# Weight granules 8 to 55 split by casting and accumulating loads from GpSimd's queue, with a ScalarE negation between

## The chip, the cores and the metric

The kernel runs on one core of one Trainium2 chip. The metric is device time in microseconds of one execution. In this document PE is the matrix engine (TensorE), PEld its weight load, DVE the vector engine (VectorE), ACT the scalar engine (ScalarE), POOL the GpSimd engine, and SP the engine (SyncE) whose queue issues the loads and stores of the kernel before.

## The reference

One decoder layer on 512 positions of width 1024, all in float32: a Mamba-2 block (`ssd_mixer`) and a sparse attention (`nsa_mixer`) side by side, an output projection with a residual, a gated feed-forward part with a short convolution, and a last RMSNorm. Cut to what matters here:

```python
h = rms_norm(x, norm1_g)
p = h @ w_in                       # 1024 x 5184: q, k, v, gates, SSM inputs
y = concat([ssd_mixer(...), rms_norm(nsa_mixer(...), attn_norm_g)])
x = x + y @ w_out                  # 2048 x 1024
u = causal_dwconv(rms_norm(x, norm2_g) @ ffn_w_up, ffn_conv_w, ffn_conv_b)
x = x + (silu(u[..., :FF]) * u[..., FF:]) @ ffn_w_down
out = rms_norm(x, final_norm_g)
```

Every product `h @ w` has to keep float32 accuracy.

## The kernel before, in words

Matmuls run on operands of type float32r. To keep the accuracy, each float32 operand `a` is split into `hi`, which is `a` written as float32r, and `lo = a - hi`, also float32r, and a product is three matmuls: hi·hi, lo·hi and hi·lo. For activations the split is made where they are computed; for weights it is made after the load.

The weights come in **granules** of 128 partitions x 1024 float32 (512 KB). The list `seq` (line 446) names 122 of them in the order of use: 0 to 39 are the input projection (`in_win`), 40 to 55 the output projection (`in_wout`), 56 to 121 the feed-forward part (`in_wup`, `in_wdn`). `w_load` (line 452) loads two granules in one 1 MB transfer on SP's queue into one of two `wr` buffers; the first two transfers go in four pieces of 256 KB between the pieces of the input. `w_split` (line 468) makes `wh` (a cast) and `wl` (a subtraction) of one granule; there are four buffers of each. `w_get` (line 483) is called by each job that multiplies with a granule, and records splits a few granules ahead.

The kernel is not written to the engines directly. Each operation is recorded (`Program.record`), and a planner (`Program.schedule`, line 284) then orders all operations with its own costs: it takes, over all engines, the operation that can start first, and among equals the one recorded first. Buffers are handed out in the order in which they were asked for. An operation recorded on `S` as a plain copy (a cast) may go to ACT or to DVE; one recorded on `DP` may go to DVE or to POOL. Line 390 is the helper that issues every planned operation, so all rows of the profile carry L390 and are told apart by their tiles. Each engine works through its own queue in the planned order, with semaphore waits for data and buffers.

The stages, by the time in the profiled execution: a start of some 40 us (granules 0 to 3, then the norm); projections with granules 4 to 11 and the compression of keys and values (40 to 100 us); attention woven with the projections of granules 12 to 39 (100 to 420 us); the SSD part woven with the first half of the output projection, tiles `on`, granules 40 to 47 (420 to 520 us); the second half, tiles `os`, granules 48 to 55 (520 to 567 us); the feed-forward part, tiles `psb` and `dn`, granules 56 to 121, to the end.

In the attention the tiles are: `pss` scores, `nm` row maxima, `p` probabilities, `l` and `rl` row sums and their inverses, `tb` transposed probabilities, `pth` and `ptl` their split, `ct` and `cp` the compressed branch, `o` the output in PSUM, `oT`, `oNh`, `oNl` the gathered and split output. `rx` and `rw` belong to the rotary embedding: `rw` is filled by four small transfers from `rx`.

The job of one output-projection half holds its four granules for four row tiles, so 2 x 4 x 3 = 24 matmuls use each granule:

```python
    def out_ssm(half):
        g0 = nxt(4)
        ws = [w_get(g0 + p_, 3 - p_) for p_ in range(4)]
        for t in range(NT):
            for g in range(2):
```

Of the kernel before, what the change touches and what calls it, by code (L numbers as in the profile page):

```python
# [10 lines left out]
F32 = mybir.dt.float32  # L11
# [8 lines left out]
P = 128  # L20
# [5 lines left out]
NEG = -1.0e30  # L26
N_SLOT = 57
N_EAGER = 3
# [135 lines left out]
class Program:  # L164


    def __init__(self, tc):
        self.tc, self.ops, self.first = tc, [], False
        self.pe, self.act, self.dve, self.pool, self.sp, self.dp = (
            _Engine(self, e) for e in ("PE", "ACT", "DVE", "POOL", "SP", "DP"))  # L170

    def buf(self, pool, shape, dt, name):
# [73 lines left out]
    def _cost(self, op, e, n, args, kw, ins, outs):  # L246
# [10 lines left out]
        if e == "ACT":  # L257
            extra = sum(isinstance(kw.get(x), View) for x in ("scale", "bias", "accum_out"))
            return ins[0].free / 1.2 + (52 if is_ps[0] else 94) + 93 * extra, TABLE.get(args[2].name, 0)
        if e in ("DVE", "POOL"):  # L260
            f = max([v.free for v in ins] + [outs[0].free])
# [21 lines left out]
    def schedule(self):  # L283
# [30 lines left out]
        while len(done) < n:  # L314
# [43 lines left out]
            if op.port.get(e):  # L358
                held[e] = op.end
            if e == "SP":  # L360
                dma_free = max(dma_free, t + 1300) + op.lat
                op.end = dma_free + 900
# [6 lines left out]
            for s in op.succ:  # L369
                s.ndep -= 1  # L370
                s.est = max(s.est, op.end + lat(e, next(iter(s.alts))))
                if s.ndep == 0:
                    push(s)
# [28 lines left out]
def layer_kernel(ctx: ExitStack, tc: tile.TileContext, x, xt, win, wdtg, wout, wup, wdn, pack, gcol, rows, cw1, consts, rot, out):  # L402
    pr = Program(tc)
    mm = pr.pe.matmul
    V, S, DP, PE, SP = pr.dve, pr.act, pr.dp, pr.pe, pr.sp

# [31 lines left out]
    raw, wh, wl = {}, {}, {}  # L438

    def w_load():  # L440
        p = st["load"]
        if 2 * p >= len(seq):
            return
        arr, i = seq[2 * p]
        raw[p] = alloc(wp, (P, 2, D), F32, f"wr{p}", "wr", 2)
        if p < 2:

            for z in range(4):
                load_x(4 * p + z)
                cs = slice(512 * (z % 2), 512 * (z % 2) + 512)  # L450
                SP.dma_start(raw[p][:, z // 2, cs], arr[p, :, z // 2, cs])
        else:
            SP.dma_start(raw[p], arr[i // 2])
        st["load"] += 1

    def w_split():
        i = st["split"]
        if i >= len(seq):
            return
        r = raw[i // 2][:, i % 2, :]  # L460
        wh[i] = alloc(wp, (P, D), F32R, f"wh{i}", "wh", 4)
        wl[i] = alloc(wp, (P, D), F32R, f"wl{i}", "wl", 4)
# [6 lines left out]
        if i % 2:  # L469
            del raw[i // 2]  # L470

    def w_get(i, ahead=2):
        while st["split"] <= i + ahead and st["split"] < len(seq):
            while st["load"] * 2 <= st["split"] + 1 and st["load"] * 2 < len(seq):
# [9 lines left out]
    def load_x(j):  # L484
        xT.append(slot(f"xT{j}"))
        SP.dma_start(xT[j], xt[j * P:(j + 1) * P])
# [11 lines left out]
    SP.dma_start(gT, gcol)  # L498
    w_load()
    ck = const("ck", (P, NCK), F32)  # L500
    SP.dma_start(ck[:, :P], consts[:, :P])
    w_load()
    SP.dma_start(ck[:, P:], consts[:, P:])
# [1078 lines left out]
```

## Time and profile before

| | |
|---|---|
| time before, median of 3 runs | 943.01 us (936.67 to 943.62) |
| the profiled execution's own time | 939.94 us |
| its span (first to last instruction) | 938.2 us, mean granted TensorE clock 0.987 |
| busy: PE / PEld / DVE / ACT / POOL | 894.1 / 727.9 / 756.8 / 408.5 / 77.4 us |
| read from HBM | 72.15 MB |

The share of busy time is an average over stages with different limits, so the tables below are read by stage. A busy PE is not a PE at its peak: matmuls are pipelined and one that waits for its operand behind others is counted as busy.

### The profile page before, as it was taken

To read this page: it belongs to the slowest core of one execution; us is meant where nothing else is said; L and a number is where in the kernel's file an instruction comes from. 1 tells how busy PE (TensorE), PEld (TensorE's weight loads), DVE (VectorE), ACT (ScalarE), POOL (GpSimd) and SP (SyncE) were. 2 spreads that over 40 slices of the span, in tenths; PEclk is the share of its full clock that TensorE was granted. 3 is DMA by queue.
4 is the path that set the end of the run, shared out by engine and by line. 5 is a ranking of instruction groups with operands and counts; after the bars stand their busy time and mean duration, and the time that the engine had idled before them with its cause. 6 is when DMAs were issued, how large, how long until landed. Compare 5 with 4: busy or idle time off the path is not lost.

```text
span 938.2 us, 12701 instructions
## 1 busy us (share of the span) xinstructions
PE 894.1 (95%) x4589; PEld 727.9 (78%) x4589; DVE 756.8 (81%) x1463; ACT 408.5 (44%) x933; POOL 77.4 (8%) x51
## 2 busy tenths in 40 slices
PE   9899889889998999999999999999999999999996
PEld 6777656767786798878777789888888888888886
DVE  7968999999999988888999678887774457777655
ACT  5434666667676677568667134312210001221013
POOL 0000222222201200010323001000000000000000
PEclk9999999999999999999999899999999999999999
DMA  9472211111111111131130222322223322222302
GB/s 308 154 202 81 72 52 56 57 51 62 46 57 57 45 45 46 46 114 56 34 136 1 90 90 90 135 90 89 90 90 99 113 101 91 90 90 93 105 28 90
DMA packets 19726, 80.82 MB, mean 86 GB/s; under 512 B 3152, under 2 KB 3920, under 8 KB 12112
## 3 DMA queue, kind: packets, MB, share of 16 engines
q1 hardware_dynamic: 19664, 80.02, 25.1%
q8 instruction: 36, 0.59, 0.3%
q14 instruction: 26, 0.21, 0.1%
HBM read 72.15 MB, written 2.10 MB: 79 GB/s over the span
## 4 chain that ended last, share of the span: by engine, by line
PE 70%; DVE 16%; ACT 6%; DMA 4%; issue 2%; SPq 1%; DVEq 0%; ACTq 0%
PE psb L390 34%; PE dn L390 13%; PE os L390 5%; PE psa L390 4%; PE tb L390 4%; PE pss L390 4%; PE o L390 3%; PE on L390 2%; DVE p L390 1%; ACT p L390 1%; DMA wr<-in_win_dram 1%; DMA rw<-rx 1%; DVE q L390 1%; SPq L390 1%; DVE ptl L390 1%
## 5 line engine op out<-in xcount | busy, mean ns | idle before, releaser
L390 PE MATMUL psb<-hTh,wh 128*128 128x512 f32 (+1 forms) x600 | 235.1, 394 | 2.3 <-ACT hTh L390 1.9
L390 PE MATMUL psb<-hTl,wh 128*128 128x512 f32 (+1 forms) x600 | 230.6, 385 | 0.0
L390 PE MATMUL psb<-hTh,wl 128*128 128x512 f32 (+1 forms) x600 | 230.4, 384 | 0.0
L390 PEld LDWEIGHTS psb<-hTh,wh 128*128 128x128 f32 x600 | 113.9, 190 | 23.3 <-ACT hTh L390 2.4
L390 DVE CAST wh<-wr 128x1024 fp32r<-128x1024 f32 (+1 forms) x80 | 53.9, 674 | 96.0 <-PE dn L390 46.5
L390 DVE TENSOR_TENSOR wl<-wr,wh 128x1024 fp32r<-128x1024 f32 (+1 forms) x105 | 124.4, 1187 | 8.2 <-ACT wh L390 2.5
L390 PEld LDWEIGHTS psb<-hTh,wl 128*128 128x128 f32 x600 | 113.4, 189 | 22.1 <-issue 0.2
L390 PEld LDWEIGHTS psb<-hTl,wh 128*128 128x128 f32 x600 | 113.6, 189 | 20.6 <-DVE hTl L390 0.4
L390 ACT ACTIVATE p<-pss,nm 128x128 f32<-128x128 f32 (+3 forms) x128 | 66.7, 524 | 45.5 <-DVE nm L390 27.5
L390 ACT ACTIVATE ug<-psb,pk 128x512 f32<-128x512 f32 x22 | 17.2, 780 | 157.6 <-PE psb L390 152.8
L390 POOL TENSOR_TENSOR wl<-wr,wh 128x1024 fp32r<-128x1024 f32 x21 | 51.2, 2440 | 360.1 <-ACT wh L390 206.5
L390 PE MATMUL dn<-wh,gTh 128*128 128x512 f32 (+1 forms) x186 | 70.5, 379 | 0.0
L390 PE MATMUL dn<-wl,gTh 128*128 128x512 f32 (+1 forms) x186 | 70.3, 378 | 0.0
L390 PE MATMUL dn<-wh,gTl 128*128 128x512 f32 (+1 forms) x186 | 70.2, 378 | 0.0
L390 ACT ACTIVATE wh<-wr 128x1024 fp32r<-128x1024 f32 (+1 forms) x46 | 47.2, 1029 | 38.2 <-PE psb L390 14.2
L390 PE MATMUL tb<-ck,p 128*128 128x128 f32 x320 | 52.5, 280 | 10.6 <-DVE p L390 5.6
L390 DVE TENSOR_TENSOR ptl<-tb,pth 128x512 fp32r<-128x512 f32 x80 | 54.4, 684 | 7.5 <-ACT pth L390 2.7
L390 DVE TENSOR_REDUCE nm<-pss 128x1 f32<-128x384 f32 (+3 forms) x88 | 55.7, 634 | 2.9 <-PE pss L390 2.2
L390 PEld LDWEIGHTS tb<-ck,p 128*128 128x128 f32 x320 | 38.0, 143 | 20.1 <-issue 8.2
L390 ACT ACTIVATE pth<-tb 128x512 fp32r<-128x512 f32 x58 | 34.3, 594 | 18.6 <-PE tb L390 15.7
L390 PEld LDWEIGHTS dn<-wh,gTh 128*128 128x128 f32 x186 | 35.0, 188 | 7.4 <-DVE xr L390 1.0
L390 PEld LDWEIGHTS dn<-wh,gTl 128*128 128x128 f32 x186 | 35.0, 188 | 6.5
(316 smaller groups left out, 1685.8 us busy)
## 6 DMA issues: line engine op xcount, KB each, us to landing
wr<-in_wup_dram SPq DMA_DIRECT2D x22, 1024.0 KB, 4.8
wr<-in_win_dram SPq DMA_DIRECT2D x18, 1024.0 KB, 4.9
wr<-in_wdn_dram SPq DMA_DIRECT2D x11, 1024.0 KB, 4.7
wr<-in_wout_dram SPq DMA_DIRECT2D x8, 1024.0 KB, 4.8
rw<-rx SPq DMA_DIRECT2D x56, 64.0 KB, 2.0
xT<-in_xt_dram SPq DMA_DIRECT2D x8, 256.0 KB, 4.7
wr<-in_win_dram SPq DMA_DIRECT2D x8, 256.0 KB, 4.8
xr<-in_x_dram SPq DMA_DIRECT2D x8, 256.0 KB, 3.6
```

The costliest lines, as they stand in the source:

```text
L390: getattr(engines[op.eng], name)(*[real(a) for a in args], **{k: real(v) for k, v in kw.items()})
```

## The change: granules 8 to 55 by loads that cast and add

For granules 8 to 55 (`by_dma`) two loads on POOL's queue replace the load on SP's queue and both engine operations. The first load writes `wh` straight from HBM and casts float32 to float32r on the way. ACT then writes `wl = -wh` (Identity with scale -1). The second load reads the same 512 KB from HBM again and adds it to `wl`, which gives w - hi. Granules 0 to 7 and 56 to 121 are still split by the engines, but in halves of 512 columns, each loaded by a transfer of its own (256 KB) into a slot of the general pool instead of the two `wr` buffers. Buffers of `wh` and `wl` go from four to seven each, the general pool from 57 to 54 slots, and splits of granules 8 to 55 are recorded at least three ahead. The planner learns to plan a load on POOL's queue.

```diff
+N_WH = 7
+N_WL = 7
+AHEAD = 3
+LOOK = 2
+D0, D1 = 8, 56
...
+    def by_dma(i):
+        return D0 <= i < D1
+
     def w_load():
...
+        if by_dma(i):
+            wh[i] = alloc(wp, (P, D), F32R, f"wh{i}", "wh", N_WH)
+            PD.dma_start(wh[i], arr[j // 2, :, j % 2])
         else:
-            SP.dma_start(raw[p], arr[i // 2])
+            for z in range(2):
+                if i < 4:
+                    load_x(2 * i + z)
+                raw[i, z] = slot("wr")
+                SP.dma_start(raw[i, z], arr[j // 2, :, j % 2, 512 * z:512 * z + 512])
         st["load"] += 1
 
     def w_split():
...
-        n = 512 if i < 4 else D
-        for c0 in range(0, D, n):
-            cs = slice(c0, c0 + n)
-            S.activation(wh[i][:, cs], r[:, cs], AF.Copy)
-            DP.tensor_sub(wl[i][:, cs], r[:, cs], wh[i][:, cs].bitcast(F32))
+        if by_dma(i):
+            S.activation(wl[i], wh[i].bitcast(F32), AF.Identity, scale=-1.0)
+            PD.dma_start(wl[i], arr[j // 2, :, j % 2], accum_op=ALU.add)
+        else:
+            wh[i] = alloc(wp, (P, D), F32R, f"wh{i}", "wh", N_WH)
+            for z in range(2):
+                cs = slice(512 * z, 512 * z + 512)
+                r = raw.pop((i, z))
+                S.activation(wh[i][:, cs], r, AF.Copy)
+                DP.tensor_sub(wl[i][:, cs], r, wh[i][:, cs].bitcast(F32))
...
     def w_get(i, ahead=2):
+        ahead = max(ahead, AHEAD) if by_dma(i + 1) else ahead
...
-        while st["load"] < st["split"] // 2 + 2 and st["load"] * 2 < len(seq):
+        while st["load"] <= st["split"] + LOOK and st["load"] < len(seq):
             w_load()
```

How the planner's order moves is shown at three places. The numbers behind the names are buffer numbers; the number within `wh24` or `wl24` is the granule.

First, POOL in the attention. Before, its queue holds the subtractions of granules 22 to 25, with one small operation of the compressed branch (`cp`) between:

```order
L390 TENSOR_TENSOR wl22_1860<-wr11_1476,wh22_1818 128x1024
L390 TENSOR_TENSOR cp_1788<-cp_1788,ck_125 128x128
L390 TENSOR_TENSOR wl23_1991<-wr11_1476,wh23_1926 128x1024
L390 TENSOR_TENSOR wl24_2116<-wr12_1732,wh24_2073 128x1024
L390 TENSOR_TENSOR wl25_2273<-wr12_1732,wh25_2245 128x1024
```

Now the same stretch of POOL's queue holds two loads for each granule:

```order
L400 DMA wh24_1702<-in_win_dram 128x1024
L400 DMA wl24_1763<-in_win_dram 128x1024
L400 DMA wh25_1856<-in_win_dram 128x1024
L400 DMA wl25_1915<-in_win_dram 128x1024
L400 DMA wh26_1968<-in_win_dram 128x1024
```

Over the whole program POOL now issues 96 loads, and its subtractions for weights go from 21 of 1024 columns to 15 of 512, all of granules 0 to 7 and 56 on.

Second, DVE in the attention, where two scalings of probabilities by `rl` stand. Before:

```order
L390 RECIPROCAL rl_1309<-l_1249 128x4
L390 TENSOR_REDUCE nm_1313<-pss_1232 128x1
L390 TENSOR_TENSOR rl_1309<-rl_1309,gates_696 128x4
L390 SCALAR_TENSOR_TENSOR xbc_1299<-psb_1164,pk_225,xbc_1299 128x511
L390 TENSOR_SCALAR p_1248<-p_1248,rl_1309 128x256
L390 TENSOR_SCALAR p_1297<-p_1297,rl_1309 128x256
```

Now:

```order
L400 RECIPROCAL rl_1348<-l_1239 128x4
L400 TENSOR_REDUCE nm_1352<-pss_1302 128x1
L400 TENSOR_TENSOR q2_1346<-rx_1167,q2_1346 64x512
L400 TENSOR_TENSOR rl_1348<-rl_1348,gates_708 128x4
L400 SCALAR_TENSOR_TENSOR xbc_1273<-psb_1196,pk_233,xbc_1273 128x511
L400 TENSOR_SCALAR p_1238<-p_1238,rl_1348 128x256
L400 TENSOR_SCALAR p_1330<-p_1330,rl_1348 128x256
```

DVE's order around the scalings is nearly the same. Over the whole program DVE loses the casts and subtractions of granules 8 to 55, and takes from ACT 14 scalings of `p` and 7 copies of `z`, while ACT takes 7 casts of `pth` from DVE and 48 negations.

Third, PE in the second half of the output projection (tiles `os0`, `os1`), where granule 55, the last of its job, is first used. Before, its six matmuls for row tile 0 stand together behind those of granule 54:

```order
L390 MATMUL os0_5898<-wl54_5878,hTh_402 128x512
L390 MATMUL os0_5898<-wh54_5869,hTl_412 128x512
L390 MATMUL os0_5898<-wh55_5882,hTh_402 128x512
L390 MATMUL os0_5898<-wl55_5892,hTh_402 128x512
L390 MATMUL os0_5898<-wh55_5882,hTl_412 128x512
```

Now the first of them is followed by work for other row tiles, and the first use of `wl55` stands 23 matmuls later:

```order
L400 MATMUL os0_5983<-wl54_5898,hTh_405 128x512
L400 MATMUL os0_5983<-wh54_5778,hTl_405 128x512
...
L400 MATMUL os0_5983<-wh55_5924,hTh_405 128x512
L400 MATMUL os1_5993<-wh52_5691,hTh_405 128x512
L400 MATMUL os1_5993<-wl52_5747,hTh_405 128x512
...
L400 MATMUL os2_6015<-wh52_5691,hTl_405 128x512
L400 MATMUL os0_5983<-wl55_5978,hTh_405 128x512
L400 MATMUL os0_5983<-wh55_5924,hTl_405 128x512
```

The buffer of `wh55` is that of granule 48, whose last use stands 60 matmuls ahead of that first use of `wl55`.

## Rows read from the trace of the kernel before

**Rows 1.** Windows by stage: each engine's busy us, instructions; clock, DMA share, GB/s

```profile
core 0: us, PE busy (x) PEld busy (x) DVE busy (x) ACT busy (x) POOL busy (x), PEclk, DMA share, GB/s
0.00:40.00 40.00, 34.88 (x141) 25.93 (x142) 34.86 (x73) 21.92 (x45) 0.20 (x4) 0.96 0.78 271
40.00:100.00 60.00, 56.03 (x269) 45.49 (x268) 48.51 (x120) 24.22 (x53) 2.40 (x1) 1.00 0.46 132
100.00:420.00 320.00, 300.14 (x1729) 238.85 (x1726) 290.92 (x605) 212.63 (x540) 48.69 (x24) 0.99 0.17 55
420.00:520.00 100.00, 92.50 (x546) 74.89 (x546) 96.29 (x218) 70.93 (x173) 23.67 (x22) 0.97 0.15 54
520.00:590.00 70.00, 69.75 (x380) 60.23 (x381) 51.51 (x113) 22.27 (x38) 2.41 (x1) 0.96 0.29 101
590.00:900.00 310.00, 309.98 (x1368) 256.32 (x1367) 212.86 (x272) 46.67 (x64) 0.00 (x0) 1.00 0.27 97
```

**Rows 2.** The same windows, only instructions that read the loaded weights `wr`

```profile
40.00:100.00 60.00, 11.78 (x11) 4.85 (x5) 2.40 (x1) 1.00 0.46 132
100.00:420.00 320.00, 16.27 (x16) 22.64 (x22) 42.92 (x18) 0.99 0.17 55
420.00:520.00 100.00, 5.43 (x6) 7.27 (x7) 3.51 (x2) 0.97 0.15 54
```

**Rows 3.** Groups by shape, whole span: count, busy us, mean ns, idle before

```profile
L390 DVE TENSOR_TENSOR wl<-wr,wh 128x1024 fp32r<-128x1024 f32 x97 | 119.0, 1228 | 7.9 <-ACT wh L390 2.3 <-DVE wh L390 0.5
L390 DVE CAST wh<-wr 128x1024 fp32r<-128x1024 f32 x75 | 51.8, 691 | 94.7 <-PE dn L390 46.5 <-PE psb L390 43.9 <-issue 2.5
L390 ACT ACTIVATE wh<-wr 128x1024 fp32r<-128x1024 f32 x43 | 45.4, 1058 | 37.9 <-PE psb L390 14.2 <-issue 12.0 <-PE on L390 4.2
L390 DVE CAST gTh<-uv 128x512 fp32r<-128x512 f32 x21 | 9.0, 426 | 0.7
L390 DVE TENSOR_TENSOR wl<-wr,wh 128x512 fp32r<-128x512 f32 x8 | 5.5, 682 | 0.3 <-ACT wh L390 0.3
```

**Rows 4.** Timeline of POOL, one of 18 such in 100 to 420 us: start, us

```profile
128.42 2.37 POOL L390 TENSOR_TENSOR wl<-wr,wh 128x1024 fp32r<-128x1024 f32 x1 [4.40 <-ACT wh L390]
```

**Rows 5.** Timeline of DVE, 100 to 420 us

```profile
101.56 2.29 DVE L390 CAST q<-rx 64x512 fp32r<-64x512 f32 x1
...
128.71 2.49 DVE L390 TENSOR_SCALAR p<-p,rl 128x256 f32<-128x256 f32 x2
...
137.80 1.08 DVE L390 TENSOR_SCALAR p<-p,rl 128x384 f32<-128x384 f32 x3
...
161.83 0.49 DVE L390 TENSOR_SCALAR p<-p,rl 128x512 f32<-128x512 f32 x1
...
176.52 3.42 DVE L390 TENSOR_SCALAR p<-p,rl 128x512 f32<-128x512 f32 x3
...
419.59 2.63 DVE L390 TENSOR_SCALAR p<-p,rl 128x512 f32<-128x512 f32 x3
```

**Rows 6.** Chain of work that ended last, in order of time: start, us, what

```profile
101.63 2.21 DVE q L390
...
176.60 3.33 DVE p L390 x3
...
419.59 1.85 DVE p L390
...
521.23 33.92 PE os L390 x140
```

**Rows 7.** Groups of PE by shape: psb in 100 to 420 us, then in 600 to 700

```profile
L390 PE MATMUL psb<-hTh,wh 128*128 128x512 f32 x152 | 65.0, 427 | 0.3 <-ACT p L390 0.2
...
L390 PE MATMUL psb<-hTl,wh 128*128 128x512 f32 x147 | 57.2, 389 | 0.0
```

**Rows 8.** DMA issues: operation, count, KB each, median us from issue to landing

```profile
wr<-in_wout_dram SPq DMA_DIRECT2D x8, 1024.0 KB, 4.8
xr<-in_x_dram SPq DMA_DIRECT2D x8, 256.0 KB, 3.6
```

More of the change, by code (lines that the diff above doesn't have):

```diff
@@ L26 @@
 NEG = -1.0e30
-N_SLOT = 57
+N_SLOT = 54
+N_WH = 7
[3 more added lines that the diff above has]
+D0, D1 = 8, 56
 N_EAGER = 3
@@ L170, in __init__ @@
             _Engine(self, e) for e in ("PE", "ACT", "DVE", "POOL", "SP", "DP"))
+        self.dma_free = 0.0
     def buf(self, pool, shape, dt, name):
@@ L259, in _cost @@
             return ins[0].free / 1.2 + (52 if is_ps[0] else 94) + 93 * extra, TABLE.get(args[2].name, 0)
+        if n == "dma_start" and e == "POOL":
+            v = outs[0]
+            op.lat = v.ids.shape[0] * v.free * 4 / (180.0 if "accum_op" in kw else 360.0)
+            return 1000.0, 0
         if e in ("DVE", "POOL"):
@@ L359, in schedule @@
                 held[e] = op.end
-            if e == "SP":
-                dma_free = max(dma_free, t + 1300) + op.lat
+            if op.lat:
+                dma_free = max(dma_free, t + 1300 + (1000 if e == "POOL" else 0)) + op.lat
                 op.end = dma_free + 900
@@ L370, in schedule @@
                 s.ndep -= 1
-                s.est = max(s.est, op.end + lat(e, next(iter(s.alts))))
+                s.est = max(s.est, op.end + (0.0 if op.lat else lat(e, next(iter(s.alts)))))
                 if s.ndep == 0:
@@ L404, in layer_kernel @@
     mm = pr.pe.matmul
[L405 removed]
+    V, S, DP, PE, SP, PD = pr.dve, pr.act, pr.dp, pr.pe, pr.sp, pr.pool
     cp = ctx.enter_context(tc.tile_pool(name="cp", bufs=1))
@@ L438, in layer_kernel @@
     raw, wh, wl = {}, {}, {}
+    def by_dma(i):
+        return D0 <= i < D1
     def w_load():
-        p = st["load"]
-        if 2 * p >= len(seq):
+        i = st["load"]
+        if i >= len(seq):
             return
[L444 to L451, printed above, removed]
-        else:
-            SP.dma_start(raw[p], arr[i // 2])
+        arr, j = seq[i]
+        if by_dma(i):
+            wh[i] = alloc(wp, (P, D), F32R, f"wh{i}", "wh", N_WH)
+            PD.dma_start(wh[i], arr[j // 2, :, j % 2])
+        else:
+            for z in range(2):
[3 more added lines that the diff above has]
+                SP.dma_start(raw[i, z], arr[j // 2, :, j % 2, 512 * z:512 * z + 512])
         st["load"] += 1
@@ L459, in w_split @@
             return
-        r = raw[i // 2][:, i % 2, :]
-        wh[i] = alloc(wp, (P, D), F32R, f"wh{i}", "wh", 4)
-        wl[i] = alloc(wp, (P, D), F32R, f"wl{i}", "wl", 4)
-        n = 512 if i < 4 else D
-        for c0 in range(0, D, n):
-            cs = slice(c0, c0 + n)
-            S.activation(wh[i][:, cs], r[:, cs], AF.Copy)
-            DP.tensor_sub(wl[i][:, cs], r[:, cs], wh[i][:, cs].bitcast(F32))
+        arr, j = seq[i]
+        wl[i] = alloc(wp, (P, D), F32R, f"wl{i}", "wl", N_WL)
+        if by_dma(i):
[8 more added lines that the diff above has]
+                DP.tensor_sub(wl[i][:, cs], r, wh[i][:, cs].bitcast(F32))
         st["split"] += 1
-        if i % 2:
-            del raw[i // 2]
     def w_get(i, ahead=2):
+        ahead = max(ahead, AHEAD) if by_dma(i + 1) else ahead
         while st["split"] <= i + ahead and st["split"] < len(seq):
-            while st["load"] * 2 <= st["split"] + 1 and st["load"] * 2 < len(seq):
+            while st["load"] <= st["split"] and st["load"] < len(seq):
                 w_load()
             w_split()
-        while st["load"] < st["split"] // 2 + 2 and st["load"] * 2 < len(seq):
+        while st["load"] <= st["split"] + LOOK and st["load"] < len(seq):
             w_load()
@@ L499, in layer_kernel @@
     w_load()
+    w_load()
     ck = const("ck", (P, NCK), F32)
     SP.dma_start(ck[:, :P], consts[:, :P])
+    w_load()
     w_load()
```

## The prediction

> **What bounds the kernel now.** I read the windows by stage first. From 590 us on PE is busy 309.98 of 310 us and issues a matmul each 0.227 us (310 us over 1368) [rows 1]: nothing that feeds PE there can make this part faster, it can only make it slower. The room is in the three stretches before 520 us. In 100 to 420 us PE is busy 300 of 320 us, so 20 us are open, and some of the busy time is waiting too: a `psb` matmul has a mean of up to 427 ns there and 389 ns in the feed-forward part [rows 7]; over 152 of them that alone is 6 us. So PE could give back 26 us or a little more in this stretch and no more. What stands beside it is DVE: 291 of 320 us busy, and in 420 to 520 us 96.3 of 100 [rows 1].
>
> Second, the same windows for the instructions that read `wr`, which are the splits: in 100 to 420 us they cost DVE 16.3 us, ACT 22.6 us and POOL 42.9 us (18 subtractions) [rows 2]. POOL looks free at 48.7 of 320 us, so its share seems to cost nothing. Third, the timelines of POOL and DVE side by side show that it does. POOL's subtraction runs from 128.42 to 130.79 us [rows 4]. DVE starts two scalings of `p` at 128.71 us, and they are over at 131.20 us: 2.49 us for what takes 2 x 0.36 = 0.72 us when POOL is idle (three longer ones take 1.08 us) [rows 5]. DVE counts this as busy. Last, the chain of waits: such stretched pieces are on it, seven between the `q` at 101.63 and the `p` at 419.59 us [rows 6].
>
> The sum is made against the profiled execution's own 939.94 us, which is 1.7 us over its span and 3.1 us under the median of the three runs.
>
> **Attention, 100 to 420 us: what goes.** The 18 subtractions on POOL go, and with them the stretched DVE pieces. Four of them: the `q` cast at 101.56 us took 2.29 us where a cast of 512 columns takes 0.43 us [rows 3, 5], so 1.86 us too much; the two `p` at 128.71 us 1.77; the three at 176.52 us 3.42 - 3 x 0.49 = 1.95; the three at 419.59 us 2.63 - 1.47 = 1.16 [rows 5]. The mean is 1.69 us. Seven pieces of this kind lie on the chain of waits in the stretch, so 7 x 1.69 = 12 us. I take -12. If PE or ACT takes the place at once, it is 0; at most it is PE's 26.
>
> DVE's own 16.3 us of splits go too. Against it the planner's order puts 14 scalings of `p` on DVE (0.36 to 0.49 us each [rows 5], some 6 us) and 7 copies. ACT loses 22 casts and gets 28 negations; the nearest row is its cast of 1024 columns at 1058 ns [rows 3], so ACT goes up by 6 x 1.06 = 6 us and is 213 of 320 us busy now [rows 1]: its idle time covers that. Without that cover it costs the 6 us. Of what is left of DVE's 16.3 I take -2, with -14 and +6 as ends.
>
> **The second stretch, 420 to 520 us.** DVE is 96% busy and its splits are 5.4 us, POOL's two are 3.5 us [rows 1, 2]. POOL keeps its operations of the SSD part, and they now stand in one queue with loads that wait for PE to free a buffer, so some of the gain may be given back there. I take -3, with -5.4 and +3 as ends.
>
> **40 to 100 us.** DVE's splits are 11.8 of 48.5 busy us in 60 us [rows 1, 2]. The compression's small transfers share the DMA engines with twice the weight bytes, but no longer stand behind a 1 MB load in SP's queue. I take -2, with -5 and +3 as ends.
>
> **The start.** From 0 to 40 us the DMA engines are 78% busy at 271 GB/s [rows 1]. The loads of granule 8 now come ahead of granules 4 to 7 in the plan's order: 0.5 MB at 271 GB/s is 1.9 us, and with granule 9 and one second load three times that. I take +1.5, with 0 and +5.8 as ends.
>
> **Does a granule come in time?** A granule's way is now a load, a negation, a second load. No row shows either load. By the nearest ones, 256 KB land after 3.6 us and 1 MB after 4.8 us [rows 8]; I take 4.2 us for the first, and for the second, which moves its bytes in and reads what it adds to, between 4.2 and 2 x 4.8 = 9.6 us; with 1.06 us of negation between them the way is 9.5 to 14.9 us. I take 11, near the landing of 1 MB. In the attention a granule is used each 320 / 28 = 11.4 us, and seven buffers let it start some six uses ahead, so it is hidden many times over. The tight place is 520 to 567 us, where 24 matmuls use a granule; at 0.242 us each (33.92 us over 140) [rows 6] that is 5.8 us. Granule 55 waits for the buffer of granule 48, and in PE's order 60 matmuls stand between that buffer's last use and the first need of `wl55`: 60 x 0.242 = 14.5 us. That is over 11 and about the upper end, so I take 0, with +3 for that place and its like at granule 51.
>
> The Trainium skill, in "DMA: Bandwidth & Descriptors", section "Anatomy of one DMA", fits a load issued from GpSimd as 2.0 us plus its bytes at 436 GB/s. By it a granule's load would be an estimated 3.2 us and the way 7.5 us, and the wait at granule 55 would be 0 as well; no row here shows such a load.
>
> **Feed-forward part.** 66 granules are now split in halves: two casts and two subtractions of 512 columns are 2 x (0.43 + 0.68) = 2.2 us against 0.69 + 1.23 = 1.9 us [rows 3], so 0.3 us more each, 20 us in all, on a DVE that is idle 97 of 310 us and an ACT that is idle 263 [rows 1]. PE hides it: 0. Without that cover it would be the 20 us.
>
> **The sum.** -12 - 2 - 3 - 2 + 1.5 = -17.5 us: 939.94 - 17.5 = 922.4, so 922 us. DVE remains the busiest after PE; what is late next are the plain dependences between scores, maxima, exponentials and transposes.
>
> **The rivals.** *The freed time is taken up elsewhere.* Attention is one long chain of PE, DVE and ACT steps, and where DVE's stretched piece goes, ACT may be late, since it now has the negations. For it: DVE stays above 85% busy, having got scalings from ACT. Against it: the pieces are on the chain one by one. Then only some 4 us are left, a third of the -12, and the time is 936 us.
>
> *POOL's loads hold DVE up as its subtractions did.* POOL has to do something for each load it issues, and there are 56 issues in the attention where there were 18 subtractions. Beside them, 11 DVE pieces from 101.56 to 419.59 us [rows 5] took 17 us too long in sum, 0.95 us for each subtraction, and 12 of the 17 lay on the chain. If an issue cost as much, DVE would lose 56 x 0.95 = 53 us, of which 53 x 12 / 17 = 37 on the chain: the -12 becomes +25, and with the other terms the time is 939.94 + 25 - 5.5 = 959 us. All of the gain is eaten from 0.44 us an issue on (56 x 0.44 x 12 / 17 = 17.5 us). For it: 2.37 us is what POOL held DVE for when it worked on a granule, whatever it did. Against it: an issue moves no 1024 columns through POOL. Beside this mechanism stands the Trainium skill, "SBUF — State Buffer", section "Who interferes with whom": GpSimd and some DVE modes contend for one pair of ports, "the other fully blocks"; the stretched pieces agree with that, at 2.49 us for 0.72 [rows 4, 5]. The same page, section "SBUF: two separate sides", says that DVE can keep GpSimd from writing the descriptors of its loads, so the loads would be late instead; no row of this kernel shows it.
>
> *The adding loads are slow.* 48 pairs of loads lie between about 50 us and 552 us of the new time. From 502 / 48 = 10.5 us of DMA time for a pair they set the pace, and each us more costs 48. At 11.2 us a pair: 922 + 34 = 956 us. For it: nothing shows the rate of an adding load. Against it: the DMA engines are 17% busy in this part at 55 GB/s [rows 1], and doubled bytes would leave them under a half.
>
> **Chances.** The forecast 0.65, with a range of its own of 912 to 932 us; freed time taken up, 0.19; POOL's issues hold DVE up, 0.10; slow adding loads, 0.06. A measurement of this kernel can tell about 1% (9.4 us) from no change. The forecast is nearly all faster by that (0.62, with 0.03 within 1%), the second case nearly all within 1% (0.02 faster, 0.17 within), the last two slower but for 0.02. So faster 0.64, same 0.22, slower 0.14. The range leaves out most of the two slow cases and the edge of the first: 908 to 944 us.
>
> **What would show it.** Right: in 100 to 420 us no DVE piece of `p`, `oNl` or `rl` takes more than its usual time, DVE's splits are gone, and the same work ends some 14 us earlier; from there to the end nothing moves but the offset. Wrong: PE waits for `wl` or `wh` with a DMA as the one that ends the wait; DVE pieces stretched beside POOL's issues; a landing of the second load beyond 10 us; or a feed-forward part longer than now, with PE waiting for `wh` from DVE.

## The result and the profile after

The changed kernel takes 931.89 us (median of 8 runs, 929.52 to 934.61), the kernel before beside it 939.2 us (8 runs, 936.19 to 943.62): a ratio of 0.9924, interval 0.9895 to 0.9952. It is faster by 7.3 us. The forecast was 922 us, a gain of 17.5 us; the time lies in the range, but more than half of the forecast gain did not come.

The profiled execution took 934.61 us (span 932.8, before 938.2), 5.3 us less than that of before. To see where, I cut both traces at the same points in PE's timeline: the first `psb`, the first `tb` (transposed probabilities), the last `o`, the first and the last `os`, the last `dn`. So a stretch is not one of the fixed windows of [rows 1], and the times that name it are those of the kernel before. The lengths in us between these marks, and what the prediction had for each:

| stretch | before | after | difference | predicted |
|---|---|---|---|---|
| start, to the first `psb` | 34.3 | 34.8 | +0.5 | +1.5 |
| to the first `tb` (40 to 100 us) | 78.0 | 85.2 | +7.2 | -2 |
| attention, to the last `o` | 317.2 | 300.6 | -16.7 | -14 |
| SSD part, to the first `os` | 86.9 | 86.1 | -0.8 | -3 |
| second half of the output projection, `os` | 51.0 | 55.3 | +4.2 | 0 |
| feed-forward part, to the last `dn` | 363.4 | 363.6 | +0.2 | 0 |

So the attention gave what was forecast and a little more, and two places that had been taken as free or as a small gain gave 11.4 us of it back. The windows by stage of the changed kernel, in the columns of [rows 1]:

```profile
0.00:40.00 40.00, 34.23 (x138) 25.10 (x139) 31.82 (x68) 22.07 (x43) 8.09 (x12) 0.96 0.91 284
40.00:100.00 60.00, 54.44 (x244) 43.49 (x244) 40.97 (x110) 28.17 (x61) 15.32 (x19) 0.97 0.80 190
100.00:420.00 320.00, 309.54 (x1791) 249.07 (x1789) 272.38 (x617) 221.74 (x546) 48.51 (x64) 0.98 0.47 105
420.00:520.00 100.00, 94.03 (x548) 75.98 (x548) 89.86 (x227) 66.03 (x163) 26.43 (x32) 0.98 0.64 174
520.00:590.00 70.00, 66.22 (x367) 57.12 (x366) 46.00 (x104) 26.00 (x47) 13.44 (x12) 0.98 0.51 159
590.00:900.00 310.00, 310.00 (x1369) 256.59 (x1368) 201.17 (x324) 75.66 (x119) 2.58 (x2) 1.00 0.19 62
```

In 100 to 420 us DVE is down from 290.9 to 272.4 us and PE up from 300.1 to 309.5, with 1791 matmuls recorded in place of 1729: they stand closer together. The price is in the DMA column: 0.17 became 0.47 there, 0.15 became 0.64 in the SSD part, and 0.46 became 0.80 in 40 to 100 us. No instruction that reads `wr` is left in the attention or the SSD part, which answers to [rows 2]:

```profile
100.00:420.00 320.00, 0.00 (x0) 0.00 (x0) 0.00 (x0) 0.98 0.47 105
420.00:520.00 100.00, 0.00 (x0) 0.00 (x0) 0.00 (x0) 0.98 0.64 174
```

What took its place, in the groups by shape (columns of [rows 3]), is a negation as dear as the cast that it was priced by (1054 against 1058 ns), and POOL's issues of 0.59 and 0.88 us. The splits in halves cost 712 and 426 to 631 ns:

```profile
L400 ACT ACTIVATE wl<-wh 128x1024 fp32r<-128x1024 f32 x48 | 50.5, 1054 | 27.3 <-DMA wh<-in_win_dram 16.2 <-DMA wh<-in_wout_dram 11.1
L400 POOL DMA_DIRECT2D wh<-in_win_dram x32 | 18.9, 590 | 100.8 <-PE psb L400 83.7 <-PE psa L400 11.9 <-issue 4.4
L400 POOL DMA_DIRECT2D wl<-in_win_dram x32 | 28.1, 877 | 162.6 <-ACT wl L400 147.8 <-ACT p L400 6.7 <-ACT ct L400 5.3
L400 DVE TENSOR_TENSOR wl<-wr,wh 128x512 fp32r<-128x512 f32 x133 | 89.9, 712 | 16.9 <-ACT wh L400 16.9
L400 ACT ACTIVATE wh<-wr 128x512 fp32r<-128x512 f32 x80 | 49.8, 631 | 199.8 <-PE psb L400 97.9 <-PE dn L400 66.5 <-issue 12.3
L400 DVE CAST wh<-wr 128x512 fp32r<-128x512 f32 x68 | 28.9, 426 | 91.2 <-PE psb L400 43.7 <-PE dn L400 39.6 <-issue 2.7
```

Do the issues hold DVE up as the subtractions did [rows 4, 5]? The timelines of POOL and of DVE at one place in the attention, POOL's first:

```profile
181.07 0.72 POOL L400 DMA_DIRECT2D wh<-in_win_dram  x1 [8.40 <-PE psb L400]
...
412.86 0.74 POOL L400 DMA_DIRECT2D wh<-in_wout_dram  x1 [1.79 <-PE psa L400]
```

```profile
181.19 0.47 DVE L400 TENSOR_SCALAR p<-p,rl 128x512 f32<-128x512 f32 x1
...
412.61 1.67 DVE L400 TENSOR_SCALAR p<-p,rl 128x512 f32<-128x512 f32 x4
```

They don't. The scaling at 181.19 us runs inside POOL's issue and takes its usual 0.47 us; the four at 412.61 us take 0.42 each. The same shapes over the whole stretch: the scaling of 512 columns had a mean of 688 ns before and has 483 now, the `q` cast 728 and 418. Before:

```profile
L390 DVE TENSOR_SCALAR p<-p,rl 128x512 f32<-128x512 f32 x17 | 11.0, 688 | 0.2
L390 DVE CAST q<-rx 64x512 fp32r<-64x512 f32 x6 | 4.4, 728 | 0.1
```

and after:

```profile
L400 DVE TENSOR_SCALAR p<-p,rl 128x512 f32<-128x512 f32 x20 | 8.7, 483 | 0.2
L400 DVE CAST q<-rx 64x512 fp32r<-64x512 f32 x7 | 2.9, 418 | 0.2
```

PE's own `psb` matmuls in the attention hardly changed, 426 ns against the 427 of [rows 7]:

```profile
L400 PE MATMUL psb<-hTh,wh 128*128 128x512 f32 x156 | 66.4, 426 | 0.0
```

The 6 us of hidden waiting that I had read into that row were not what the gain came from. What went is in good part PE's idle time: between the two marks of the attention it was 19.7 us before and is 10.4 us now. PE's waits for DVE fell from 16.9 to 3.1 us in sum, and its waits for ACT rose from 2.3 to 7.0. The costliest wait before (what PE waited for: us in total, times, longest us), which the list after no longer has:

```profile
PE tb L390 <- DVE p L390: 5.6, 4, 2.2
```

Now the two places that lost. The chain of waits of the changed kernel before the attention, and then at the end of the `os` stage (start, us, what), read as in [rows 6]:

```profile
53.93 6.26 DMA rw<-rx
...
64.06 10.16 DMA x2b<-rx
74.24 6.87 DMA x2b<-vcr
...
85.59 5.15 DMA rw<-rx
...
529.64 0.55 POOL wh L400
...
537.47 7.35 DMA wl<-in_wout_dram
544.87 4.09 PE os L400 x10
```

The first four are small copies between buffers on the chip, the rotary's `rw` and the compression's `x2b`, 28.4 us in sum. Before, the same part of the chain (34 to 112 us) held five such copies, 16.8 us in sum:

```profile
52.87 7.03 DMA x2a<-vcr
59.92 2.15 DMA x2b<-rx
...
63.95 2.29 DMA x2a<-vcr
...
81.10 1.78 DMA rw<-rx
...
87.97 3.50 DMA rw<-rx
```

So the copies alone take 11.7 us more of the chain; the stretch lost 7.2. The DMA issues (count, KB each, median us from issue to landing) answer to [rows 8]:

```profile
wh<-in_win_dram POOLq DMA_DIRECT2D x32, 512.0 KB, 3.9
wl<-in_win_dram POOLq DMA_DIRECT2D x32, 512.0 KB, 5.5
wh<-in_wout_dram POOLq DMA_DIRECT2D x16, 512.0 KB, 5.2
wl<-in_wout_dram POOLq DMA_DIRECT2D x16, 512.0 KB, 7.4
rw<-rx SPq DMA_DIRECT2D x56, 64.0 KB, 3.2
```

The median of `rw` was 2.0 us before; that of all `x2a` and `x2b` was 5.0 and 2.6 us before and is 8.0 and 7.4 now (the landings of one tile, least, median and most, first `x2a`, then `x2b`):

```profile
DMA to landing us min/median/max: 5.8/8.0/9.5
DMA to landing us min/median/max: 5.0/7.4/10.2
```

And in the `os` stage PE waits for a load, 4.1 us in two waits (1.97 us at 514.06 us and 2.16 at 544.87), which are those for granules 51 and 55:

```profile
L400 PE MATMUL os<-wl,hTh 128*128 128x512 f32 x64 | 26.8, 419 | 4.1 <-DMA wl<-in_wout_dram 4.1
```

The waits are not their whole price. Right behind each, PE's granted clock is 0.51 and 0.54, the lower of its two levels (1.2 GHz; 2.4 is the upper), in the columns of [rows 1]:

```profile
514.00:517.50 3.50, 3.44 (x8) 2.79 (x9) 0.86 (x3) 0.11 (x1) 0.00 (x0) 0.51 1.08 275
544.80:548.50 3.70, 3.63 (x9) 2.91 (x10) 0.75 (x1) 0.25 (x1) 0.00 (x0) 0.54 0.00 0
```

There a matmul starts every 0.43 us, in the rest of the stage every 0.23. That is some 1.7 us more behind each wait, 3.3 us in sum, so that the two waits cost some 7.4 us together. The stage before has one such stretch too (granted clock 0.76 in 516 to 530 us), behind PE's waits for DVE.

### The profile page after: what moved, and what is told of

The parts are those of the page before. It is cut to its first block, busy times and chain, and to the rows that moved or that the text cites. A ratio compares the mean times of both kernels' runs of the same rounds, so it can differ in the third digit from the quotient of the medians.

```text
span 932.8 us, 13270 instructions
## 1 busy us (share of the span) xinstructions
PE 894.0 (96%) x4589; PEld 729.5 (78%) x4589; DVE 696.5 (75%) x1502; ACT 447.0 (48%) x994; POOL 114.4 (12%) x139
## 4 chain that ended last, share of the span: by engine, by line
PE 70%; DVE 9%; issue 6%; DMA 6%; ACT 6%; POOL 2%; SPq 1%; DVEq 0%; POOLq 0%; ACTq 0%
PE psb L400 34%; PE dn L400 13%; PE psa L400 6%; PE pss L400 5%; PE tb L400 4%; PE o L400 4%; DMA rw<-rx 2%; PE on L400 2%; ACT p L400 1%; SPq L400 1%; ACT ct L400 1%; DMA x2b<-rx 1%; DVE hTl L400 1%; POOL wl L400 1%; DMA wl<-in_wout_dram 1%
## 5 line engine op out<-in xcount | busy, mean ns | idle before, releaser
L400 ACT ACTIVATE wh<-wr 128x512 fp32r<-128x512 f32 x80 | 49.8, 631 | 199.8 <-PE psb L400 97.9
L400 DVE TENSOR_TENSOR wl<-wr,wh 128x512 fp32r<-128x512 f32 x133 | 89.9, 712 | 16.9 <-ACT wh L400 16.9
L400 DVE CAST wh<-wr 128x512 fp32r<-128x512 f32 x68 | 28.9, 426 | 91.2 <-PE psb L400 43.7
L400 ACT ACTIVATE p<-pss,nm 128x128 f32<-128x128 f32 (+3 forms) x128 | 66.8, 525 | 36.9 <-DVE nm L400 17.6
L400 PE MATMUL dn<-wh,gTh 128*128 128x512 f32 (+1 forms) x186 | 70.3, 378 | 0.0
L400 ACT ACTIVATE wl<-wh 128x1024 fp32r<-128x1024 f32 x48 | 50.5, 1054 | 27.3 <-DMA wh<-in_win_dram 16.2
L400 POOL TENSOR_TENSOR wl<-wr,wh 128x512 fp32r<-128x512 f32 x15 | 20.6, 1382 | 227.8 <-ACT wh L400 186.6
L400 ACT ACTIVATE pth<-tb 128x512 fp32r<-128x512 f32 x65 | 38.5, 596 | 19.9 <-PE tb L400 17.3
L400 POOL DMA_DIRECT2D wl<-in_win_dram x32 | 28.1, 877 | 162.6 <-ACT wl L400 147.8
```

Of the source, the lines that this page charges most:

```text
L400: getattr(engines[op.eng], name)(*[real(a) for a in args], **{k: real(v) for k, v in kw.items()})
```

## The experiments

Theory after the result: POOL's subtractions were the price in the attention, and their end is the gain; what is given back is given back by the adding loads, by their bytes in 40 to 112 us and by their latency in the `os` stage. The rivals are in the expectations. All but two edits are to the changed kernel; each run is compared with the kernel before on the same chip. That kernel's median moved from 939.2 to 942.1 us between these comparisons, so runs are set against one another by their ratios rather than by a few us. In each, the stretches are those of the first table, as differences from the kernel before, in us, in that order up to `os`. They come from one profiled execution of each and move by a few us where the planner's order changes, so the sum over a kernel counts for more than one stretch.

| run | start | to `tb` | attention | SSD | `os` | time, us | ratio, interval |
|---|---|---|---|---|---|---|---|
| the change | +0.5 | +7.2 | -16.7 | -0.8 | +4.2 | 931.89 | 0.9924 (0.9895 to 0.9952) |
| 1 `os` granules on the engines | +1.7 | +8.5 | -16.5 | +6.1 | -2.0 | 936.28 | 0.9957 (0.9943 to 0.9971) |
| 2 first 16 on the engines | +4.7 | +0.5 | -20.3 | -0.6 | +3.5 | 931.36 | 0.9914 (0.9892 to 0.9936) |
| 3 second load plain | +0.4 | +6.9 | -19.7 | -1.5 | -2.5 | 922.98 | 0.9816 (0.9796 to 0.9835) |
| 4 second load cut, 8 to 15 | +0.5 | +0.9 | -17.6 | -1.0 | +1.7 | 927.15 | 0.9861 (0.9839 to 0.9883) |
| 5 layout only | +4.5 | -3.1 | -6.8 | +6.7 | -1.5 | 939.98 | 0.9979 (0.9962 to 0.9996) |
| 6 before, 8 to 55 not on POOL | +1.9 | +0.3 | -11.0 | +1.1 | +1.6 | 930.72 | 0.9877 (0.9852 to 0.9901) |
| 7 51 and 55 on the engines | +0.9 | +7.8 | -18.0 | -0.9 | -3.7 | 926.23 | 0.9824 (0.9800 to 0.9849) |
| 8 as 7, loads from 12 on | +6.1 | +5.8 | -16.0 | -0.6 | -2.8 | 933.47 | 0.9909 (0.9887 to 0.9931) |
| 10 as 7, five buffers | +3.6 | +8.0 | -20.9 | +1.4 | +3.7 | 936.53 | 0.9954 (0.9932 to 0.9976) |
| 11 as 7, no weights on POOL | -0.1 | +4.9 | -19.7 | -1.3 | -2.6 | 925.59 | 0.9841 (0.9804 to 0.9877) |
| 12 as 9 and 11 | -0.2 | +11.2 | -16.3 | -1.3 | -4.2 | 930.00 | 0.9894 (0.9857 to 0.9931) |
| 13 as 11, loads from 16 on | +4.7 | +0.9 | -16.8 | -1.1 | -3.2 | 923.87 | 0.9831 (0.9803 to 0.9859) |
| 14 before, none on POOL | -0.2 | -1.3 | -12.0 | +1.1 | -0.3 | 927.59 | 0.9875 (0.9853 to 0.9897) |

Run 9 (925.89 us; 0.9839, 0.9799 to 0.9878) has no row: nothing is read from its trace.

### What POOL's subtractions cost: runs 6, 14 and 5

Run 6 is the kernel before with one word changed; run 14 has `V` for all granules.

```diff
-            DP.tensor_sub(wl[i][:, cs], r[:, cs], wh[i][:, cs].bitcast(F32))
+            (V if 8 <= i < 56 else DP).tensor_sub(wl[i][:, cs], r[:, cs], wh[i][:, cs].bitcast(F32))
```

> The kernel before, but the subtractions of granules 8 to 55 may go to DVE alone. Theory (POOL's subtractions hold DVE up by 17 us in the attention, 12 of them on the chain): those pieces are back at their usual time, DVE gets 18 x 1.23 = 22 us of subtractions instead, so the attention stays within 5 us of 317 us and the total at 936 to 944 us. Rival (the collisions lie off the path and only DVE's and POOL's own time counts): the attention grows by 10 us or more, total 948 us or above. Rival (only the collisions count): the attention is 8 us shorter or more, total 932 us or below.

> The kernel before with all subtractions of weights on DVE, none on POOL. Theory (POOL's subtractions are the main cost that the change takes away; DVE then carries 20 us more of splits in the attention, and some 5 us more in the SSD part, which the loads spare it): like the kernel that kept POOL's subtractions only outside granules 8 to 55, 929 to 932, slower than the loads with granules 51 and 55 on the engines (about 926). Rival (the loads bring nothing beyond what taking POOL's subtractions away brings): 924 to 927.

Measured: 930.72 and 927.59 us. The attention is 11 to 12 us shorter though DVE now carries all its splits; in run 14, 37.5 us where [rows 2] have 16.3 (the windows, instructions that read `wr`, DVE and ACT):

```profile
100.00:420.00 320.00, 37.51 (x32) 24.28 (x23) 0.99 0.17 56
```

The scalings are back at their usual time, and PE waits little for them (run 14, DVE's group in 100 to 420 us, then PE's wait in the attention):

```profile
L390 DVE TENSOR_SCALAR p<-p,rl 128x512 f32<-128x512 f32 x21 | 9.1, 482 | 0.2
...
PE tb L390 <- DVE p L390: 1.3, 2, 0.8
```

21 us more work on the busiest engine after PE, and the stretch is 12 us shorter: that is the price of 18 subtractions on POOL, and it is at least the 12 us of the forecast, though the planner's order moves a little with the edit too. In run 6 the theory fell, and the rival by which only the collisions count came true on both marks (11.0 us shorter, 930.72); run 14 lies between its two expectations. Without one adding load both kernels are as fast as the changed one or faster (0.9877 and 0.9875 against 0.9924; only the edges of the intervals overlap). The rest of the attention's gain, 16.7 - 12.0 = 4.7 us, may be what the loads add by freeing DVE of splits; the change also has seven buffers and halves in place of whole granules, and no run takes these apart.

Run 5 takes the change without the loads, all granules split in halves:

```diff
-D0, D1 = 8, 56
+D0, D1 = 8, 8
```

> No granule is split by the loads; halves of 512 columns in slots of the general pool, seven buffers of wh and wl and 54 slots stay. Theory (the gain of the attention comes from what the loads take off POOL and DVE): the attention, from the first transposition to the last matmul of tile o, stays at 312 to 322 us as in the kernel before (317 us), the total is 937 us or above. Rival (the deeper buffers alone bring the gain): the attention takes 305 us or less, the total is 930 us or below.

Measured 939.98 us, within 0.4% of before, so the layout by itself brings nothing in the whole. Its parts are not nothing: it costs 4.5 us at the start, loses 6.7 in the SSD part, and the attention, at 310.5 us, is 6.8 us shorter, which neither expectation had (312 to 322, or 305 and less). POOL still had 41 subtractions of 512 columns there, and the scalings of 512 columns had a mean of 591 ns, between the 688 of before and the 483 of the change. That fits shorter subtractions that collide less, but the deeper buffers are in this kernel too.

### What the adding costs: runs 3 and 4

```diff
+            if "accum_op" in kw:
+                kw = {}
```

In run 3 the second load is issued as a plain one, in the same planned order, so the addition is left out and `wl` holds the weight itself.

> The second load of granules 8 to 55 writes the weights over wl and adds nothing, so the addition is left out; the order of all instructions and the bytes from HBM are those of the changed kernel. Theory A (adding makes the second load slow): its landing falls from 5.5 and 7.4 us to that of the first load, 4 to 5 us, the two waits for granules 51 and 55 shrink by 2 us each, and the total is 926 to 929 us. Theory B (it lands late because it queues behind other transfers, adding is free): landing within 0.5 us of the changed kernel's, total 931 to 933 us.

Measured 922.98 us, ratio 0.9816 against the change's 0.9924: theory A, and 3 us more than it forecast. The bytes read from HBM are the same; the second load lands in 3.9 and 4.5 us where the adding one took 5.5 and 7.4, and PE's wait in the `os` stage is 0.8 us:

```profile
wl<-in_win_dram POOLq DMA_DIRECT2D x32, 512.0 KB, 3.9
wl<-in_wout_dram POOLq DMA_DIRECT2D x16, 512.0 KB, 4.5
...
L402 PE MATMUL os<-wl,hTh 128*128 128x512 f32 x64 | 25.1, 393 | 0.8 <-DMA wl<-in_wout_dram 0.8
```

But the first `tb` is as late as in the change. So the adding itself makes the waits in the `os` stage; the loss before the attention is not made by the adding but, if by the loads at all, by their bytes. Run 4 tests that: the second load of granules 8 to 15 moves 32 of 1024 columns (the rest of those `wl` stays the negation), in the same order.

```diff
+            if "accum_op" in kw and int(args[0].buf.name[2:]) < 16:
+                args = [v[:, :32] for v in args]
```

> The second load of granules 8 to 15 is cut to 32 of 1024 columns, so most of the addition for these granules is left out; order and waits are those of the changed kernel. Theory (traffic of the second loads delays the compression's transfers): the small transfers x2a and x2b land in 5 to 6 us at the median instead of 7 to 9, the first transposition of the attention comes 3 to 5 us earlier than the changed kernel's 120 us, total 927 to 929 us. Rival (the first loads, the order or DVE in the start make the delay): within 1 us of the changed kernel, 931 to 933 us.

Measured 927.15 us, as the theory had it, and the first `tb` came 6.3 us earlier than in the change where it had 3 to 5. The stretch up to the first `tb` lost 0.9 us in place of 7.2, and `x2a` and `x2b` land in a median of 5.1 and 4.3 us:

```profile
DMA to landing us min/median/max: 2.2/5.1/5.4
DMA to landing us min/median/max: 3.2/4.3/5.7
```

### The early loss, other ways: runs 2 and 8 to 13

If the bytes before the attention are the trouble, leaving those loads out, spreading them or holding them back should help. Run 2 has `D0, D1 = 16, 56`; run 8 has `D0 = 12` and granules 51 and 55 on the engines.

> Granules 8 to 15 are split by the engines, 16 to 55 by the loads. Theory (the doubled weight traffic and the loads of granules 8 to 15 delay the compression's small transfers, 7.7 us by the first transposition of the attention): the first transposition comes within 2 us of the kernel before (112.3 us) and the total is 924 to 927 us. Rival (the delay comes from the new layout in halves and the new order of the start): the first transposition still comes 5 us or more late, and the total stays at 930 us or above.

> As the kernel before it in this list, and granules 8 to 11 are split by the engines too, so half of the adding loads that run beside the compression's small transfers are gone. Theory: the first transposition of the attention comes 3 to 4 us earlier than in the changed kernel (120 us), total 923 to 927 us. Rival (what the loads gave comes back as engine work in the start, as with 8 to 15): the first transposition within 2 us of the changed kernel's, total 928 us or above.

Run 2 took away the stretch's loss (+0.5) and paid 4.7 us for it at the start. So by its own marks the rival came true: the first `tb` was still 5.1 us late (117.44 us against 112.30), and the time 931.36 against 924 to 927. Run 8 missed wholly: 933.47. In runs 9 and 12 the negations of granules 11 to 15 stand behind the compression's reads of `x2a` and `x2b`, in 10 there are five buffers, and in 11 to 13 the engines' subtractions are on DVE alone:

```diff
+    for op in cxs[:12]:
+        pr.order(op, [neg[i] for i in range(11, 16)])
     pr.schedule()
```

```diff
-N_WH = 7
-N_WL = 7
+N_WH = 5
+N_WL = 5
```

```diff
-                DP.tensor_sub(wl[i][:, cs], r, wh[i][:, cs].bitcast(F32))
+                V.tensor_sub(wl[i][:, cs], r, wh[i][:, cs].bitcast(F32))
```

> The kernel with granules 51 and 55 split by the engines, whose first transposed probabilities start 8.7 us later than before the change, and in addition the negations of granules 11 to 15 stand on ACT behind the compression's reads of x2a and x2b for the keys, so that their adding loads can't run while the x2a and x2b transfers do. Theory (the adding loads' bytes delay the compression's transfers): x2a and x2b land in 3 to 5 us, the first tb starts 2 to 4 us later than before the change, and the time falls by 4 to 6 us, to 920 to 922. Rival (what is late is the order of the projections and the layout of the loads, and the missing bytes of the cut loads helped in another way): first tb stays at +7 to +9, time within 2 us of 926.

> The same kernel, without the hold, and with five buffers each of wh and wl in place of seven. Theory (seven free buffers let loads of seven granules start within 20 us): with five the burst from 40 to 80 us is smaller, the first tb starts 4 to 6 us later than before the change in place of 8.7; the second half of the output projection, which holds four granules, waits for wl again by 4 us or more, so the time is about the same, 925 to 929. Rival (buffers don't set the burst): first tb stays at +8 to +9 and the time is 928 to 932 by the waits alone.

> The same kernel with seven buffers, and the subtractions of the granules that the engines split only on DVE, none on POOL. Theory (POOL's subtractions of 512 columns hold DVE up at the start as those of 1024 did in the attention): the stretched hTl and hTh pieces go, psb starts 0 to 2 us earlier, and the time falls by 1 to 2 us, to 924 to 925. Rival (at the start DVE is short of time, and POOL's help is worth its price): psb starts 1 to 3 us later and the time is 927 to 929.

> Both edits together: adding loads of granules 11 to 15 held behind the compression's reads, and subtractions of engine-split granules only on DVE. Theory: the two gains add up, 918 to 921. Rival: the start's loss and the hold's gain cancel, 924 to 927.

> The kernel with granules 51 and 55 split by the engines and all engine subtractions on DVE, and in addition granules 8 to 15 split by the engines. Theory (the early loss is the traffic of the loads of granules 8 to 15, and the start's loss of earlier kernels of this layout is POOL's subtractions): psb starts within 1 us of the kernel before, x2a and x2b land in 3 to 5 us, the first tb starts 0 to 2 us later than before the change in place of 4.9 to 8.7, and the time is 920 to 923. Rival (16 granules split in halves cost the start on DVE what the loads cost later): the first tb stays at +4 or more and the time is 925 to 929.

Holding the loads back is no gain: run 9 is not told apart from run 7 (0.9839 and 0.9824, intervals overlap), and run 12, at 930.00 us, missed both its expectations. Its trace shows the transfers landing early again, yet the stretch up to the first `tb` is the longest of all, +11.2 us (`x2a`, then `x2b`, run 12):

```profile
DMA to landing us min/median/max: 2.4/4.6/6.5
DMA to landing us min/median/max: 2.2/5.5/6.3
```

The compression came earlier (its first `cps` matmul at 70.3 us against 76.7) and the queries later: PE's first score matmuls then waited for DVE's `q`, 4.6 us in three waits. Behind the longest, 3.33 us at 112.28 us, the granted clock was 0.50, the 1.2 GHz level, in 113 to 124 us, where the change has 1.00 in 113 to 121. So transfers that land early are not enough by themselves: the hold also moved the planner's order, and how the loss divides between the order, the waits and the clock was not taken apart. Five buffers were worse (936.53): the stretch up to `tb` stayed at +8.0, the waits for `wl` came back, 5.5 us of PE in the `os` stage, and the start lost 3.6 us. That is the rival, and some 4 us beyond it.

Run 11 shows that POOL's subtractions of 512 columns stretched DVE's `hTl` early on: in the changed kernel one `hTl` piece took 2.37 us at 45.64 us, beside POOL's subtraction of 1.58 us at 45.87, and the eight pieces in 30 to 60 us had a mean of 978 ns; with the subtractions on DVE it is 685 ns, and the first `psb` comes 1.0 us earlier than in run 7. The total, 925.59, is not told apart from run 7's 926.23.

Run 13 bears out the first half of its theory and not the second. With the loads of granules 8 to 15 gone, the stretch to `tb` lost 0.9 us, as in runs 2 and 4, and `x2a` lands in a median of 2.3 us; but the start lost 4.7 us with no subtraction on POOL, against the expectation of less than 1, so the first `tb` itself is 5.5 us late, which is the rival's mark. Its time, 923.87, lies between the two expectations. Three kernels that load granules 8 to 15 in halves lost 4.5 to 4.7 us at the start (runs 2, 5, 13), and what they save later is paid there in good part. POOL's subtractions are not the cause; what is stays open.

### The `os` stage: runs 1 and 7

Run 1 splits granules 48 to 55 by the engines (`D0, D1 = 8, 48`), run 7 only two of them:

```diff
-        return D0 <= i < D1
+        return D0 <= i < D1 and i not in (51, 55)
```

> Granules 48 to 55 are split by the engines again, 8 to 47 stay with the loads. Theory (the second half of the output projection lost 4.2 us because granules 51 and 55 came late): no wait of PE for a DMA of weights in the os stage, the os stage 3 to 5 us shorter than in the changed kernel, total 927 to 929 us. Rival (the os stage is longer for another reason, the norm's chain or DVE): the os stage stays within 1 us of the changed kernel's and the total at 931 to 933 us.

> The changed kernel, but granules 51 and 55, the last of the two jobs of the os stage, are split by the engines. Theory (these two come late because load, negation and adding load follow one another after a late buffer): PE's two waits for an adding load in the os stage go, the os stage is 3 to 4 us shorter, total 927 to 930 us. Rival (another granule's adding load takes their place): the waits stay at 3 us or more, total 931 to 933 us.

Both took away PE's waits for a DMA in the stage, and in run 7 the granted clock with them stays at the upper level (first the group, then the window of the stage):

```profile
L400 PE MATMUL os<-wl,hTh 128*128 128x512 f32 x64 | 25.0, 391 | 0.0
...
506.00:554.00 48.00, 47.48 (x224) 38.99 (x223) 34.94 (x87) 19.16 (x40) 4.33 (x6) 1.00 0.75 239
```

The stage went from 55.3 to 49.0 us in run 1 and to 47.3 in run 7: 8.0 us less, of which the two waits and the lower clock behind them are some 7.4. But run 1 lost 6.1 us in the SSD part, where its extra splits and loads then stand: a load of half a granule is on the chain, with two of ACT's casts of 0.63 us right behind it:

```profile
476.92 5.15 DMA wr<-in_wout_dram
```

At 936.28 it is slower than the change; the expectation was right on the waits and wrong on the total. Run 7, with two granules in place of eight, keeps the SSD part at -0.9 and takes 926.23 us, ratio 0.9824: it beats the kernel before and the change. Run 13 is as good (0.9831). Against run 14's 0.9875, which needs no loads on POOL's queue, run 7 is 0.5% better and run 13 0.4%; the intervals of 13 and 14 overlap, and those of 7 and 14 lie 0.0004 apart.

## Why the prediction was right or wrong

**Attention: right, by its mechanism.** -14 was predicted and -16.7 came. DVE's pieces are back at their usual time (483 ns for 688), and runs 6 and 14 show the cause by itself: with POOL's weight subtractions moved to DVE and the loads left as they were, 11.0 and 12.0 us go. How the 16.7 divide between the -12 and the -2 of the sum is not shown: the 12.0 are what is left after 21 us more work on DVE. That the freed time would be taken up by ACT (the first rival) happened in part only: PE waits 13.8 us less for DVE there and 4.7 us more for ACT, about a third of it, where the rival had two thirds. (That rival's 936 us leaves the other terms out; with their -5.5 it would have been 930.)

**"POOL's loads hold DVE up as its subtractions did": fell.** An issue of 0.72 us runs beside a DVE scaling that takes its usual 0.47 us, and over 100 to 420 us the scalings of 512, 384 and 256 columns have means of 483, 415 and 348 ns with the loads on POOL and of 482, 415 and 348 ns in run 14 without them. The rule of the Trainium skill that was set beside this rival ("SBUF — State Buffer", "Who interferes with whom") agrees with the subtractions, but no DVE piece shown here is blocked by the issue of a load.

**40 to 100 us: the step that failed.** The prediction took -2, "with -5 and +3 as ends", and wrote that the small transfers "share the DMA engines with twice the weight bytes, but no longer stand behind a 1 MB load". Measured: +7.2. The two halves of that sentence were weighed by which queue the transfers wait in, not by how busy the engines behind the queues are. With seven buffers free, loads run at once: the DMA share went from 0.46 to 0.80, `x2b` from a median of 2.6 to 7.4 us, and the copies on the chain take 28.4 us in place of 16.8. Run 4 shows the bytes of the second loads of granules 8 to 15 to be the cause, and runs 2 and 13, without these granules' loads, agree: the stretch's loss is then 0.5 to 0.9 us.

**"Does a granule come in time?": the other step that failed.** The place and the +3 were named, and 0 was taken because 14.5 us of cover stood against a way of 11. Both were mis-sized. For granule 55 the way was 15.2 us by the trace: first load issued at 529.64, negation at 536.11, adding load issued at 537.47, landed 7.35 us later at 544.82 us. That is 0.3 us over the upper end of 14.9: the first load took some 6.4 us until the negation could start, not the 4.2 taken, and 0.3 us passed between the negation's end and POOL's issue, which the sum had not. The cover was 13.1 us, from the first issue at 529.64 to 542.71, where PE began to wait: the 0.242 us for a matmul were a mean with a stretch at the lower clock in it, and at the 0.227 us seen here 60 of them are 13.6 us, counted from the buffer's last use, a little ahead of POOL's issue. So PE waited 2.16 us there, and 1.97 us at granule 51; the sum had no term for the lower clock behind a wait, some 1.7 us each. Runs 3 and 7 show that these waits hang on the adding load: gone with a plain load (0.8 us left) and gone with the two granules on the engines. The stage as a whole lost 4.2 us against before, which had a stretch at the lower clock of its own. The Trainium skill's fit ("DMA: Bandwidth & Descriptors", "Anatomy of one DMA"), by which a load would be an estimated 3.2 us, is below every median here: 3.9 to 5.2 us for the casting load, 5.5 to 7.4 for the adding one.

**"The adding loads are slow": not as a pace.** POOL's queue moved a granule's pair in time through the attention, where PE waits for no DMA. The load was slow by latency, at two places where it had too little cover.

**The second stretch, 420 to 520 us.** -3 was predicted, -0.8 came. DVE's busy time did fall by 6.4 us (96.3 to 89.9), but PE was already busy 79.72 us of 83 in the heart of it before (the columns of [rows 1]):

```profile
430.00:513.00 83.00, 79.72 (x493) 65.37 (x493) 80.95 (x187) 59.80 (x152) 21.91 (x21) 1.00 0.13 48
```

I had bounded the attention by PE's idle time and did not do so here; PE's idle time alone was 3.3 us. Why even that did not come was not tried.

**Start and feed-forward part.** +0.5 for +1.5, and +0.2 for 0: the 20 us of extra splits in halves are hidden by PE, busy 310.00 of 310 us.

Summed: -16.7 for -14 came about as forecast; +7.2 instead of -2 and +4.2 instead of 0 make 13.4 us of the 12.2 by which the profiled executions miss the forecast sum (-5.3 for -17.5), and the other terms the rest.

## What to carry to other kernels

An engine that looks idle is not free help: 18 subtractions on POOL cost a stretch 12 us through DVE pieces that the profile counts as busy, and moving them to the busier engine, one word of code, brought at least as much as the change itself (ratio 0.9875 against 0.9924) and most of what its best variant did (0.9824). When work is moved from engines to transfers, price the transfers that are already there: here `x2a` and `x2b`, small copies on the critical path, landed in a median of 7 to 8 us in place of 3 to 5 when bigger loads ran beside them. Where a buffer comes free late and its first use is near, a way of load, negation and adding load needs its cover checked granule by granule; two granules of 48 put back on the engines brought 1.0% (ratio 0.9824 for 0.9924).

## What was not expected of the hardware

An adding load of 512 KB landed 1.6 and 2.9 us later than a plain load in the same place of the same order (5.5 for 3.9, 7.4 for 4.5 us), and POOL was busy 0.88 us with its issue where a casting load took 0.59. POOL's issues did not stretch DVE's pieces, while a subtraction of only 512 columns did. Bytes that PE had no wait for, those of the second loads of eight granules, cost 6 us (7.2 against 0.9 in run 4), while copies of 64 to 128 KB from another queue landed late beside them. And a wait of PE of 2 us for a late weight cost nearly as much again, since 3.5 us at a granted clock of 0.51 to 0.54 followed it.
